# A two-layer decoder step on one core: the MLP's up projections as one level of Strassen's product, with squared relu and residual kept in memory

## The chip, the core and the metric

The kernel runs on one core of one Trainium2 chip. The metric is the time of one execution in device microseconds (us); three runs of the kernel before took 3162.02 us in the median, 3161.73 to 3175.02. The core has five engines that work side by side and meet through semaphores: TensorE (PE in the profile, with its weight loads as PEld), VectorE (DVE), ScalarE (ACT), GpSimd (POOL) and SyncE (SP), which here only issues DMAs. On-chip data lie in SBUF; matmul results lie in PSUM, in eight banks that the program hands out as three of `pg`, three of `pm` and two of `ps2`. "Memory" below is the chip's main memory, reached by DMA.

## The reference

A step of a decoder with two layers over 1032 tokens (1024 of a prompt, 8 of running sequences), D = 1024, all in float32. Layer 0 mixes with a gated delta rule and retention, layer 1 with an SSD mixer; after each mixer stands the same MLP with a hidden width of 4096:

```python
def squared_relu_mlp(h, w1, w2):
    a = jax.nn.relu(jnp.einsum('bld,df->blf', h, w1))
    return jnp.einsum('blf,fd->bld', a * a, w2)
...
    for layer in range(DEPTH):
...
        x = x + out
        x = x + squared_relu_mlp(rms_norm(x, norm_mlp[layer]), mlp_w1[layer], mlp_w2[layer])
```

The change concerns the last line, twice: the product with w1, the squared relu, and the product with w2 onto the residual.

## The kernel before

Data lie transposed: features on the 128 partitions, the T = 1032 tokens along the free axis, in three slices of NW = 344 (`NSL`). Float32 products are made of three matmuls in a reduced format: every operand is split into a high part (a rounded copy) and a low part (the rest), and `mm3` (L146) multiplies high by high, high by low and low by high into the same bank. Weights come through `load_w` (L134): SP loads a raw tile of 128x512 (three buffers), ACT casts the high part (L142), and DVE or POOL subtracts it for the low part (L143).

`out_proj` (L1332) ends the mixer. It loads the residual from memory (`accd`) into eight tiles `acc` (L1339), adds the projection's products into them slice by slice (L1346), and with `split_piece` makes `xh` and `xl`, the high and low parts of the normed residual without its token-wise factor. That factor, rstd, is made by `rstd_from` while the first up tile runs (matmuls at L259, L279 and L295, copies on ACT at L272 and L275), and is applied after the first product, at the relu.

`mlp` (L1221) then runs 32 hidden tiles of 128 features. `up(t)` calls `gemm_tile`: 8 slices of K x 3 token slices x 3 = 72 matmuls of 344 columns into three banks, evicted by relu times rstd on DVE (L1227), the square's high part on ACT (L1228), the square itself on POOL (L1229) and its low part on DVE (L1230). The hidden tiles stay in SBUF, in 14 buffers of `a2`. After every fourth up tile (the first one counted apart) `down(b)` takes four of them through `gemm_flush`: 8 output tiles x 3 token slices x 12 = 288 matmuls of 344 columns, each slice added into `acc` by DVE (L1238). The order on each engine is the order in which these Python loops issue; nothing reorders them. An engine runs its queue in that order, and a waiting instruction holds all behind it. In layer 1 the last block is `finish`, which also does the final norm.

Of the kernel before, what the change touches and what calls it, by code (L numbers as in the profile page):

```python
# [10 lines left out]
F32 = mybir.dt.float32  # L11
# [3 lines left out]
ALU = mybir.AluOpType  # L15
# [53 lines left out]
SHF = 8  # L69
RATE = (0.5, 0.6, 1.5, 0.5, 0.6)  # L70
# [25 lines left out]
class Kern:  # L96
# [327 lines left out]
    def layer(self, l):  # L424
        tc = self.tc
        nk = 16 if l else 8
        with ExitStack() as es:
# [5 lines left out]
            self.spill = [dp.tile([P, SEQ], F32, name=f"spill{l}_{k}") for k in range(nk)]  # L433
            self.egd = dp.tile([32, SEQ], F32, name=f"egd{l}")
# [4 lines left out]
            with ExitStack() as es_op:  # L439
# [9 lines left out]
                ap = es.enter_context(tc.tile_pool(name=f"acc{l}", bufs=1, side="right", reuse_waits="tile"))  # L449
# [763 lines left out]
    def mlp(self, l, acc, last):  # L1213
        nc, tc, I = self.nc, self.tc, self.I
        with tc.tile_pool(name=f"mlp{l}", bufs=1, reuse_waits="tile") as tp:
# [3 lines left out]
            def up(t):  # L1219
                hi = tp.tile([P, T], F32R, tag="a2", name="ahi", bufs=14)  # L1220
                lo = tp.tile([P, T], F32R, tag="a2", name="alo", bufs=14)  # L1221
                parts[t] = (hi, lo)

                def ev(n, ps):
                    s = NSL[n]
                    r = tp.tile([P, NW], F32, tag="r", name="r", bufs=4)
                    nc.vector.scalar_tensor_tensor(out=r, in0=ps, scalar=0.0, in1=self.rstd_bc[:, s], op0=ALU.max, op1=ALU.mult)  # L1227
                    nc.scalar.activation(hi[:, s], r, AF.Square)  # L1228
                    nc.gpsimd.tensor_tensor(out=r, in0=r, in1=r, op=ALU.mult)  # L1229
                    nc.vector.tensor_tensor(out=lo[:, s], in0=r, in1=hi[:, s].bitcast(F32), op=ALU.subtract)  # L1230
                self.gemm_tile(I["w1"][l, t], 128, ev, t == 1)

            def down(b):
                ks = range(4 * b, 4 * b + 4)
# [8 lines left out]
                for _ in self.gemm_flush(lambda m: I["w2"][l, b, m], [parts.pop(k) for k in ks], ev):  # L1243
                    pass
            def finish(b):
# [3 lines left out]
                for m in range(KT):  # L1249
                    dst = None  # L1250
                    if m < 5:
                        w = tp.tile([P, T], F32R, tag="a2", name="wfin", bufs=14)
                        dst = (w[:, 0:512], w[:, 512:1024])
# [78 lines left out]
    def out_proj(self, name, blocks, acc, tp, parts, norm):  # L1332
# [3 lines left out]
        with tc.tile_pool(name="oq" + name, bufs=1, side="right", reuse_waits="tile") as tq:  # L1336
# [3 lines left out]
            for i in range(1, len(blocks)):  # L1340
# [3 lines left out]
                def ev(m, n, ps):  # L1344
                    o = acc[m][:, NSL[n]]
                    nc.vector.tensor_tensor(out=o, in0=o, in1=ps, op=ALU.add)  # L1346
                    if last:
                        self.split_piece(m, n, o, ssq, tp, norm)
# [563 lines left out]
```

## Time and profile before

| what | value |
|---|---|
| median of three runs | 3162.02 us |
| the profiled execution | 3163.67 us, span in the trace 3161.5 us |
| TensorE clock granted over the span | 0.972 |
| MLP of layer 0 in the trace | about 779 to 1509 us |
| MLP of layer 1 in the trace | from about 2412 us nearly to the end |

The profile shows one execution. Its first part gives each engine's busy time and share of the span; the second cuts the span into 40 slices and gives busy tenths. The windows view gives, for chosen stretches, each engine's busy time with the number of instructions that began there, then the TensorE clock granted, the DMA engines' busy share and GB/s. In rows of groups the numbers are the count, busy time, mean duration in ns, then idle time before them with its releaser. A source view gives the least, middle and greatest duration of one line's instructions in ns.

### The profile page before, as it was taken

How to read it: one execution, taken by the hardware profiler on the slowest of the kernel's cores; microseconds unless marked ns; L12 is line 12 of the kernel's file. 1: busy time of each engine (PE TensorE's matmuls, PEld its weight loads, DVE VectorE, ACT ScalarE, POOL GpSimd, SP SyncE). 2: the span in 40 equal slices, each digit the busy share in tenths (PEclk: the TensorE clock that was granted, in tenths of full speed). 3: DMA queues.
4: the chain of work that ended last, by engine and by line, in shares of the span. 5: the costliest groups of instructions: out<-in, count | busy, mean ns of one | idle time of the engine just before them, and what ended most of it. 6: DMA issues, size and time to landing. Idle time of an engine off the chain costs nothing. (4 is left out here: it accounts for less than half of the span.)

```text
span 3161.5 us, 48870 instructions
## 1 busy us (share of the span) xinstructions
PE 3039.6 (96%) x19702; PEld 2918.4 (92%) x19702; DVE 1672.0 (53%) x3191; ACT 830.1 (26%) x1573; POOL 914.0 (29%) x928
## 2 busy tenths in 40 slices
PE   8999999989999999999998999998899999999998
PEld 6888888878999999999997989898899999999998
DVE  7664657554333333334788696968435333333334
ACT  4222222213211111113343434343124111111112
POOL 2121114114222112224135445445224222221124
PEclk9899989889999999999999999999999999999999
DMA  4011103153111111112222232324721111111112
GB/s 128 21 49 55 48 22 109 56 179 107 44 47 47 47 47 47 47 47 77 73 66 76 74 103 76 96 75 136 255 74 44 47 47 47 47 47 47 47 47 71
DMA packets 119186, 223.32 MB, mean 71 GB/s; under 512 B 14064, under 2 KB 43504, under 8 KB 118960
## 3 DMA queue, kind: packets, MB, share of 16 engines
q1 hardware_dynamic: 110512, 190.80, 19.9%
q0 software_dynamic: 8448, 29.40, 2.4%
q8 instruction: 155, 2.54, 0.3%
q14 instruction: 71, 0.58, 0.1%
HBM read 174.78 MB, written 43.24 MB: 69 GB/s over the span
## 5 line engine op out<-in xcount | busy, mean ns | idle before, releaser
L148 PE MATMUL pg<-xh,whi 128*128 128x344 f32 x3072 | 1000.9, 326 | 6.2 <-DVE z L1495 3.2
L150 PE MATMUL pg<-xh,wlo 128*128 128x344 f32 x3072 | 997.5, 325 | 0.7 <-DVE wlo L143 0.7
L149 PE MATMUL pg<-xl,whi 128*128 128x344 f32 x3072 | 997.1, 325 | 0.0
L148 PEld LDWEIGHTS pg<-xh,whi 128*128 128x128 f32 x3072 | 584.8, 190 | 13.0 <-DVE z L1495 3.7
L142 ACT CAST whi<-raw 128x512 fp32r<-128x512 f32 (+2 forms) x443 | 270.8, 611 | 1234.6 <-PE pg L149 1174.2
L150 PEld LDWEIGHTS pg<-xh,wlo 128*128 128x128 f32 x3072 | 584.8, 190 | 4.8 <-DVE wlo L143 1.7
L149 PEld LDWEIGHTS pg<-xl,whi 128*128 128x128 f32 x3072 | 583.6, 190 | 3.5 <-issue 2.1
L149 PE MATMUL pg<-alo,whi 128*128 128x344 f32 (+2 forms) x1476 | 472.4, 320 | 0.0
L150 PE MATMUL pg<-ahi,wlo 128*128 128x344 f32 (+2 forms) x1476 | 472.3, 320 | 0.0
L148 PE MATMUL pg<-ahi,whi 128*128 128x344 f32 (+2 forms) x1476 | 471.5, 319 | 0.0
L1238 DVE TENSOR_TENSOR acc<-acc,pg 128x344 f32<-128x344 f32 x360 | 182.9, 511 | 388.1 <-PE pg L150 388.1
L143 POOL TENSOR_TENSOR wlo<-raw,whi 128x512 fp32r<-128x512 f32 (+2 forms) x179 | 225.2, 1260 | 507.7 <-ACT whi L142 502.9
L1229 POOL TENSOR_TENSOR r<-r 128x344 f32<-128x344 f32 x192 | 146.1, 761 | 755.1 <-ACT ahi L1228 707.4
L143 DVE TENSOR_TENSOR wlo<-raw,whi 128x512 fp32r<-128x512 f32 x264 | 189.7, 719 | 190.4 <-ACT whi L142 182.6
L150 PEld LDWEIGHTS pg<-ahi,wlo 128*128 128x128 f32 x1476 | 277.6, 188 | 0.0
L148 PEld LDWEIGHTS pg<-ahi,whi 128*128 128x128 f32 x1476 | 277.5, 188 | 0.0
L149 PEld LDWEIGHTS pg<-alo,whi 128*128 128x128 f32 x1476 | 277.3, 188 | 0.0
L1230 DVE TENSOR_TENSOR alo<-r,ahi 128x344 fp32r<-128x344 f32 x192 | 134.5, 701 | 253.8 <-POOL r L1229 253.8
L1228 ACT ACTIVATE ahi<-r 128x344 fp32r<-128x344 f32 x192 | 94.5, 492 | 340.9 <-DVE r L1227 340.9
L148 PE MATMUL pg<-mhi,whi 128*128 128x344 f32 x408 | 133.2, 326 | 9.9 <-DVE acc L1346 7.1
L1227 DVE SCALAR_TENSOR_TENSOR r<-pg,rstd_bc 128x344 f32<-128x344 f32 x186 | 94.8, 510 | 79.4 <-PE pg L150 78.1
L150 PE MATMUL pg<-mhi,wlo 128*128 128x344 f32 x408 | 132.8, 326 | 0.0
(539 smaller groups left out, 4191.6 us busy)
## 6 DMA issues: line engine op xcount, KB each, us to landing
raw<-w SPq DMA_DIRECT2D x256, 256.0 KB, 2.6
raw<-wis SPq DMA_DIRECT2D x80, 256.0 KB, 2.8
raw<-wih SPq DMA_DIRECT2D x56, 256.0 KB, 2.8
mraw<-spill SPq DMA_DIRECT2D x17, 512.0 KB, 4.5
accd<-ost SPq DMA_DIRECT2D x48, 172.0 KB, 3.1
acc<-accd SPq DMA_DIRECT2D x16, 516.0 KB, 7.3
EG<-egd SPq DMA_DIRECT2D x32, 256.0 KB, 6.7
dS<-sstate SPq DMA_DIRECT2D x32, 256.0 KB, 7.1
```

Of the source, the lines that this page charges most:

```text
L142: nc.scalar.copy(hi[:, :n], raw[:, :n])
L143: (lo_eng or nc.vector).tensor_tensor(out=lo[:, :n], in0=raw[:, :n], in1=hi[:, :n].bitcast(F32), op=ALU.subtract)
L148: t.matmul(ps, lhsT=whi, rhs=xhi, start=start, stop=False)
L149: t.matmul(ps, lhsT=whi, rhs=xlo, start=False, stop=False)
L150: t.matmul(ps, lhsT=wlo, rhs=xhi, start=False, stop=stop)
L1227: nc.vector.scalar_tensor_tensor(out=r, in0=ps, scalar=0.0, in1=self.rstd_bc[:, s], op0=ALU.max, op1=ALU.mult)
L1228: nc.scalar.activation(hi[:, s], r, AF.Square)
L1229: nc.gpsimd.tensor_tensor(out=r, in0=r, in1=r, op=ALU.mult)
L1230: nc.vector.tensor_tensor(out=lo[:, s], in0=r, in1=hi[:, s].bitcast(F32), op=ALU.subtract)
L1238: nc.vector.tensor_tensor(out=s, in0=s, in1=ps, op=ALU.add)
```

## The change

The up projections of a layer are regrouped. Hidden tiles t and t + 16 form a pair; together with the two halves of K (slices 0 to 3 and 4 to 7) and with tokens cut in two halves, a pair is a product of 2x2 blocks. One level of the Strassen product in Winograd's form replaces eight block products by seven, of sums of weight blocks with sums of token blocks. Tokens are cut into four quarters of 258, so a pair is two calls of `pair`, for quarters 0 and 1 and for quarters 2 and 3, of seven products each; a product is 4 slices of K x 3 = 12 matmuls of 258 columns. Tiles 0 and 16 remain plain.

```diff
-            self.mlp(l, acc, l == 1)
+            self.mlp_up(l)
+            ap = es.enter_context(tc.tile_pool(name=f"res{l}", bufs=1, side="right", reuse_waits="tile"))
+            acc = [ap.tile([P, T], F32, name=f"res{l}_{m}") for m in range(KT)]
+            for m in range(KT):
+                nc = self.nc
+                nc.sync.dma_start(acc[m], self.accd[m])
+            self.mlp_down(l, acc, l == 1)
...
+            def out(t, cols, r, n):
+                v.scalar_tensor_tensor(out=r, in0=r, scalar=0.0, in1=self.rstd_bc[:, cols], op0=ALU.max, op1=ALU.mult)
+                a.activation(r, r, AF.Square)
+                nc.gpsimd.dma_start(self.hid[t][:, cols], r)
...
+            plain(0, False)
+            with tc.tile_pool(name=f"upx{l}", bufs=1, side="right", reuse_waits="tile") as xp:
+                for k in range(4):
+                    x = []
+                    for m in (k, k + 4):
+                        r = xp.tile([P, T], F32, tag="x", name="ux", bufs=4)
+                        nc.sync.dma_start(r, self.accd[m])
+                        a.activation(r, r, AF.Copy, scale=self.V(norm, m))
+                        x.append(quarters(r))
...
+                    for j, x0, x1, e in ((1, b12, b11, v), (2, b22, t[1], g), (3, b22, b12, v), (4, t[2], b21, g)):
+                        e.tensor_tensor(out=t[j], in0=x0, in1=x1, op=ALU.subtract)
+                    for j in (2, 1, 3, 4):
+                        hi, lo = TB[j][k]
+                        a.copy(hi, t[j])
+                        v.tensor_tensor(out=lo, in0=t[j], in1=hi.bitcast(F32), op=ALU.subtract)
+            plain(HT, True)
...
+            def weights(t):
...
+                a11, a12 = load(t, 0), load(t, 1)
+                W[1] = parts(a11)
+                W[2] = parts(a12)
+                a21 = load(t + HT, 0)
+                s3 = total(a11, a21, ALU.subtract)
+                d = total(a21, a11, ALU.subtract)
+                a22 = load(t + HT, 1)
+                s2 = total(d, a22, ALU.add)
+                W[6] = parts(s2)
+                s4 = total(a12, s2, ALU.subtract)
+                s1 = s2
+                g.tensor_tensor(out=a21, in0=a21, in1=a22, op=ALU.add)
+                W[5] = parts(a21)
+                W[7] = parts(s3)
+                W[4] = parts(a22)
+                W[3] = parts(s4)
+                return W
...
+                c1 = add(a, None, prod(1), None)
+                add(v, r0[:, L], prod(2), c1)
+                u2 = add(v, None, prod(6), c1)
+                c5 = add(a, None, prod(5), None)
+                u3 = add(v, None, prod(7), u2)
+                u4 = add(g, None, c5, u2)
+                add(g, r1[:, R], c5, u3)
+                p4 = prod(4)
+                add(v, r1[:, L], u3, p4, ALU.subtract)
+                out(t + HT, cols, r1, 516)
+                add(v, r0[:, R], prod(3), u4)
+                out(t, cols, r0, 516)
+            W = weights(1)
+            for t in range(1, HT):
+                pair(t, W, 0)
+                nxt = weights(t + 1) if t + 1 < HT else None
+                pair(t, W, 1)
+                W = nxt
```

In this diff v is DVE, a is ACT, g is POOL. `parts` casts a weight block on ACT (L1290 of the changed kernel) and subtracts for its low part on DVE (L1291); `total` is a sum on POOL (L1303; the sum into a21 is L1318). `add` with one operand copies a bank on ACT (L1340), with two it adds on the named engine (L1342). `out` is L1238 to L1240: relu times rstd on DVE over 516 tokens, square on ACT, and a store to `hid` in memory from POOL's queue. The residual takes a way through memory too: `out_proj` stores each finished `acc[m]` (L1526, SP), the token sums and, after the up stage, `res` read it back (L1262, L459).

At pair 5 hidden tiles 0 and 1 are read back and split into quarters of `xh` and `xl` that no product reads any more (L1371 to L1375). `mlp_down` begins with them: `begin` runs 8 x 4 x 6 = 192 matmuls of 258 columns, the first real block then has only two tiles, and `fetch` brings the other hidden tiles from memory (L1385), casts them on ACT (L1388) and takes their low parts on DVE (L1389), into 16 buffers of `a2`:

```diff
-            for t in range(HID):
-                up(t)
-                if t % 4 == 0 and t:
-                    down(t // 4 - 1)
+            for k in (2, 3):
+                fetch(k)
+            begin()
+            for b in range(HID // 4 - 1):
+                for k in range(4 * b + 4, 4 * b + 8):
+                    fetch(k)
+                down(b, 0 if b else 2)
```

On ACT, at the end of layer 0's output projection, `sq` being the square of the last residual piece, the queue before reads:

```order
L241 ACTIVATE sq_7562<-acc0_7_6935 128x344
L142 CAST whi_7776<-raw_7774 128x512
L272 COPY rstd_bc_70<-pm_7649 128x512
L275 COPY rstd_bc_70<-pm_7685 128x8
L272 COPY rstd_bc_70<-pm_7667 128x512
L1228 ACTIVATE ahi_7570<-r_7688 128x344
L1228 ACTIVATE ahi_7570<-r_7705 128x344
```

and now (`ux` is the residual read back, `sa` a token sum, `t10h` to `t40h` their high parts, `r` the hidden tile 0):

```order
L242 ACTIVATE sq_7601<-acc0_7_6967 128x344
L143 CAST whi_7934<-raw_7932 128x512
L1263 ACTIVATE ux_7798<-ux_7798,vec_68 128x1032
L1263 ACTIVATE ux_7801<-ux_7801,vec_68 128x1032
L273 COPY rstd_bc_70<-pm_7720 128x512
L276 COPY rstd_bc_70<-pm_7756 128x8
L1271 CAST t10h_7611<-sa_7804 128x516
L1271 CAST t20h_7619<-sa_7805 128x516
L273 COPY rstd_bc_70<-pm_7738 128x512
L1247 ACTIVATE r_7759<-r_7759 128x344
```

Two scalings of the residual read back have come ahead of the copies of rstd, and casts of token sums among them.

On POOL, in the middle of the up stage, a row holds the same instruction as often as xN says. Before, around a down block, the queue has squares and low parts of weights:

```order
L1229 TENSOR_TENSOR r<-r 128x344 x8
L143 TENSOR_TENSOR wlo<-raw,whi 128x512
L1229 TENSOR_TENSOR r<-r 128x344
L143 TENSOR_TENSOR wlo<-raw,whi 128x512
L1229 TENSOR_TENSOR r<-r 128x344 x2
L143 TENSOR_TENSOR wlo<-raw,whi 128x512
L1229 TENSOR_TENSOR r<-r 128x344
L143 TENSOR_TENSOR wlo<-raw,whi 128x512 x5
```

Now, for the pair 5 (`c` and `r` are the parts of its outputs, `sa` and `raw` the weight sums of pair 6):

```order
L1342 TENSOR_TENSOR c<-c 128x258
L1342 TENSOR_TENSOR r<-c 128x258
L1303 TENSOR_TENSOR sa<-raw 128x512 x2
L1240 DMA hid_21_128<-r 128x516
L1240 DMA hid_5_112<-r 128x516
L1303 TENSOR_TENSOR sa<-sa,raw 128x512
L1318 TENSOR_TENSOR raw<-raw 128x512
L1303 TENSOR_TENSOR sa<-raw,sa 128x512
```

The squares and low parts are gone from POOL; the sums of the next pair's weights stand between the output sums and the stores of the pair at hand.

On SP, at the end of the up stage, loads have come that were not there: the residual, and hidden tiles between the weights of w2. Before, SP loads only weights there.

```order
L1298 DMA raw<-w 128x512 x31
L139 DMA raw<-w 128x256 x6
L459 DMA res_0_12075<-accd_0_140 128x1032
L459 DMA res_1_12076<-accd_1_141 128x1032
L459 DMA res_2_12077<-accd_2_142 128x1032
```

Behind them come the other five `res` loads, then hidden tiles 2 and 3, then again weights.

More of the change, by code (lines that the diff above doesn't have):

```diff
@@ L69 @@
 SHF = 8
+A2 = 16
 RATE = (0.5, 0.6, 1.5, 0.5, 0.6)
@@ L433, in layer @@
             self.spill = [dp.tile([P, SEQ], F32, name=f"spill{l}_{k}") for k in range(nk)]
+            self.hid = [dp.tile([P, T], F32, name=f"hid{l}_{k}") for k in range(HID)]
             self.egd = dp.tile([32, SEQ], F32, name=f"egd{l}")
@@ L1214, in mlp, with mlp_down @@
+    def mlp_down(self, l, acc, last):
         nc, tc, I = self.nc, self.tc, self.I
@@ L1217, in mlp, with fetch, begin, down @@
             parts = {}
[L1219 to L1234, printed above, removed]
+            def fetch(k):
+                raw = tp.tile([P, T], F32, tag="hraw", name="hraw", bufs=2)
+                nc.sync.dma_start(raw, self.hid[k])
+                hi = tp.tile([P, T], F32R, tag="a2", name="ahi", bufs=A2)
+                lo = tp.tile([P, T], F32R, tag="a2", name="alo", bufs=A2)
+                nc.scalar.copy(hi, raw)
+                nc.vector.tensor_tensor(out=lo, in0=raw, in1=hi.bitcast(F32), op=ALU.subtract)
+                parts[k] = (hi, lo)
+            def begin():
+                for m in range(8):
+                    hi, lo = self.load_w(I["w2"][l, 0, m][:, 0:256], 256, nc.gpsimd)
+                    for j in range(4):
+                        n = slice(258 * j, 258 * j + 258)
+                        ps = self.pg()[:, :258]
+                        for k in range(2):
+                            c = slice(258 + 516 * (j % 2), 516 + 516 * (j % 2))
+                            s = slice(k * 128, k * 128 + 128)
+                            i = 2 * k + j // 2
+                            self.mm3(ps, hi[:, s], lo[:, s], self.xh[i][:, c], self.xl[i][:, c], k == 0, k == 1)
+                        nc.vector.tensor_tensor(out=acc[m][:, n], in0=acc[m][:, n], in1=ps, op=ALU.add)
+            def down(b, k0=0):
+                ks = range(4 * b + k0, 4 * b + 4)
                 def ev(m, n, ps):
@@ L1242, in ev @@
                             nc.gpsimd.dma_start(self.resd[m], acc[m])
-                for _ in self.gemm_flush(lambda m: I["w2"][l, b, m], [parts.pop(k) for k in ks], ev):
+                for _ in self.gemm_flush(lambda m: I["w2"][l, b, m][:, k0 * 128:], [parts.pop(k) for k in ks], ev):
                     pass
@@ L1251, in finish @@
                     if m < 5:
-                        w = tp.tile([P, T], F32R, tag="a2", name="wfin", bufs=14)
+                        w = tp.tile([P, T], F32R, tag="a2", name="wfin", bufs=A2)
                         dst = (w[:, 0:512], w[:, 512:1024])
@@ L1348, in ev @@
                         self.split_piece(m, n, o, ssq, tp, norm)
+                        if n == 2:
+                            nc.sync.dma_start(self.accd[m], acc[m])
                 for _ in self.gemm_flush(lambda m: self.I[name][m, :, c0 * 128:c0 * 128 + w], cur, ev):
```

79 lines of the change are left out of this document (77 added, 2 removed).

## The prediction

> **What bounds the kernel now.** I read the page's busy times and its slices first, then the windows view over the two MLP stages.
>
> ```profile
> PE 3039.6 (96%) x19702; PEld 2918.4 (92%) x19702; DVE 1672.0 (53%) x3191; ACT 830.1 (26%) x1573; POOL 914.0 (29%) x928
> ...
> PE   8999999989999999999998999998899999999998
> ```
>
> ```profile
> core 0: us, PE busy (x) PEld busy (x) DVE busy (x) ACT busy (x) POOL busy (x), PEclk, DMA share, GB/s
> 790.00:1500.00 710.00, 710.00 (x4512) 709.83 (x4513) 257.43 (x461) 142.14 (x261) 172.57 (x181) 1.00 0.17 50
> 2425.00:3095.00 670.00, 670.00 (x4261) 670.00 (x4260) 233.31 (x416) 119.04 (x212) 145.67 (x152) 1.00 0.16 46
> 900.00:1000.00 100.00, 100.00 (x638) 100.00 (x637) 33.93 (x63) 18.57 (x33) 21.28 (x23) 1.00 0.16 46
> ```
>
> TensorE is busy for all of both windows at clock 1.00, while VectorE works 36% of the first (257.43 of 710), ACT 20%, POOL 24%. Nothing but the number of matmuls and their pitch bounds the MLP. The pitch (start to start) of a matmul of 344 columns: 100 us / 638 = **156.7 ns** (the window with the most matmuls per us; missing records would only make it look longer). For fewer columns the final projection has rows:
>
> ```profile
> 3133.06 0.28 PE L148 MATMUL pg<-ahi,wfin 128*128 128x256 f32 x1
> ...
> 3135.77 0.28 PE L150 MATMUL pg<-ahi,wfin 128*128 128x256 f32 x1
> ```
>
> These are the first and last of 24 matmuls of 256 columns, each with weights of its own: 2.71 us / 23 = 117.8 ns. The slope between the two widths is (156.7 - 117.8) / 88 = 0.44 ns a column, so 258 columns cost **118.7 ns**, an estimate two columns away from a measured width.
>
> **The change on TensorE.** Before, one layer's MLP is 32 up tiles of 72 matmuls and 8 down blocks of 288, all of 344 columns: 4608 x 156.7 ns = 722.1 us. After, two up tiles stay (144 matmuls); the other 30 become 15 pairs of 2 x 7 products x 4 slices x 3 = 168 matmuls of 258. The down projection keeps 2160 matmuls of 344, and its first 144 become 192 of 258 in `begin`. Per layer 2304 x 156.7 + (2520 + 192) x 118.7 = 361.0 + 321.9 = 682.9 us: **39.2 us less**, all of it from the pairs (22.56 us before, 19.94 after, 2.6 saved, 15 times; `begin` is even: 22.8 against 22.6).
>
> **What the pairs need beside TensorE.** Durations come from these rows of the lines and source views:
>
> ```profile
> L142 ACT CAST whi<-raw 128x512 fp32r<-128x512 f32 x419 | 259.4, 619 | 1179.4 <-PE pg L149 1134.8 <-PE ps L149 14.0 <-issue 13.5
> L143 POOL TENSOR_TENSOR wlo<-raw,whi 128x512 fp32r<-128x512 f32 x155 | 202.8, 1308 | 430.4 <-ACT whi L142 425.5 <-DMA accd<-ost 4.4 <-PE pg L149 0.4
> L1754 POOL DMA_DIRECT2D o_sssm<-dS x32 | 18.5, 577 | 44.2 <-DVE dS L1753 44.2
> ```
>
> ```profile
> L143 DVE TENSOR_TENSOR wlo<-raw,whi x264: 669/692/1921, 10.1 to 3078.4; 128x512 fp32r<-128x512 f32 x132
> ...
> L143 POOL TENSOR_TENSOR wlo<-raw,whi x179: 731/1289/2292, 606.5 to 3106.2; 128x512 fp32r<-128x512 f32 x155, 128x384 fp32r<-128x384 f32 x16, 128x256 fp32r<-128x256 f32 x8
> ```
>
> ```profile
> L421 DVE SCALAR_TENSOR_TENSOR z<-th,z x48: 677/690/1529, 85.6 to 2216.0; 128x516 f32<-128x516 f32 x48
> ```
>
> ```profile
> L420 ACT ACTIVATE th<-z x48: 622/635/639, 83.8 to 2213.8; 128x516 f32<-128x516 f32 x48
> ```
>
> ```profile
> L1306 DVE TENSOR_TENSOR acc<-acc,pg x24: 410/548/564, 3101.5 to 3146.8; 128x392 f32<-128x392 f32 x8, 128x384 f32<-128x384 f32 x8, 128x256 f32<-128x256 f32 x8
> ```
>
> ```profile
> L1311 ACT ACTIVATE sqf<-acc x21: 416/525/536, 3102.6 to 3147.3; 128x392 f32<-128x392 f32 x7, 128x384 f32<-128x384 f32 x7, 128x256 f32<-128x256 f32 x7
> ```
>
> In each source row the three numbers are the least, middle and greatest duration; the least of the last two rows and of POOL's is that of 256 columns, which I take for 258. Per pair, in us:
> - DVE: seven low parts of weights 7 x 0.69, ten evictions 10 x 0.42, four relu steps of 516 columns 4 x 0.69: **11.8**.
> - ACT: seven casts 7 x 0.62, four copies 4 x 0.42, four squares 4 x 0.64: **8.6**.
> - POOL: five sums of 128x512 5 x 1.29, four of 258 columns 4 x 0.74, four DMA issues 4 x 0.58: **11.7**.
>
> Each is well under the pair's 19.9 us of TensorE. But the weights of the next pair are a chain. From the start of a pair, a product being 12 x 0.1187 = 1.42 us: products 1, 2, 6, 5, 7 end at 7.1, DVE's u3 at 7.5, POOL's r1 at 8.3; behind it POOL makes s3 and d, to 10.9; d frees the buffer of a11, the a22 load (2.6 us, row below) lands at 13.5, s2 ends at 14.8, a21+a22 at 16.1, s4 at 17.4. Weight 6 is cast and has its low part at 14.8 + 0.62 + 0.69 = 16.1, the last, weight 3, about 20 (five low parts in DVE's queue between evictions). TensorE wants weight 6 as the third product of the next pair, at 19.9 + 2.8 = 22.7, and weight 3 as its seventh, at 28.4. Over 6 us of slack: no stall, if nothing stretches. The new stores put a wait into POOL's queue: a store stands there until DVE's relu step (0.69) and ACT's square (0.64) are through, and behind it queue s2 and s4; the first half's two stores are due by 8.5 + 0.42 + 1.33 = 10.3 and 11.7, and two issues end at 12.3, before a22 has landed: covered.
>
> What may stretch it stands in the trace:
>
> ```profile
> 3096.53 1.59 DVE L1230 TENSOR_TENSOR alo<-r,ahi 128x344 fp32r<-128x344 f32 x1 [1.48 <-POOL r L1229]
> ```
>
> ```profile
> 3096.45 1.29 POOL L143 TENSOR_TENSOR wfin<-raw,wfin 128x512 fp32r<-128x512 f32 x1
> ```
>
> ```profile
> L1230 DVE TENSOR_TENSOR alo<-r,ahi x192: 504/518/1639, 793.3 to 3100.0; 128x344 fp32r<-128x344 f32 x192
> ```
>
> The DVE subtraction that began 0.08 us after a POOL one took 1.59 us where the middle one takes 0.518: it stood still nearly until POOL was through. In a pair DVE's 7 + 4 instructions on SBUF alone (7.6 us) and POOL's nine (9.4) add to 17.0 even if none overlap, under 19.9, so I add nothing in the forecast and keep the case in which the rest doesn't interleave either as a rival.
>
> The Trainium skill, "SBUF — State Buffer", section "Who interferes with whom", says that a VectorE instruction with two SBUF inputs and a GpSimd instruction that reads SBUF exclude each other for the whole instruction, and that a VectorE instruction with at most one SBUF input does not. The 1.59 us row agrees with it; by that rule every meeting in the new up stage would cost what this row shows, which is the second rival below.
>
> **Entry of the up stage (new wait).** The sums of tokens need the normed residual, which now goes to memory and back. On SP's queue each store of a piece waits for its last add; the weight loads of both plain tiles stand ahead of the last store, behind it only loads for the first pair and the loads back. Rows for it:
>
> ```profile
> L259 PE MATMUL pm<-ones_r,rstd_bc x54: 212/275/317, 779.7 to 2414.9; 128*128 128x56 f32 x54
> ```
>
> ```profile
> L272 ACT COPY rstd_bc<-pm x8: 586/587/588, 47.0 to 2424.3; 128x512 f32<-128x512 f32 x8
> ```
>
> ```profile
> L1228 ACT ACTIVATE ahi<-r 128x344 fp32r<-128x344 f32 x192 | 94.5, 492 | 340.9 <-DVE r L1227 340.9
> ```
>
> ```profile
> acc<-accd SPq DMA_DIRECT2D x16, 516.0 KB, 7.3
> ...
> resd<-acc POOLq DMA_DIRECT2D x8, 516.0 KB, 4.1
> ```
>
> ```profile
> raw<-w SPq DMA_DIRECT2D x256, 256.0 KB, 2.6
> ```
>
> ```profile
> L226 ACT ACTIVATE xh<-xr,vec x8: 1139/1156/1158, 6.1 to 23.5; 128x1032 fp32r<-128x1032 f32 x8
> ```
>
> Count from the last add of the output projection. The last residual piece is stored (4.1 us), and by the program's semaphores the second load back waits for it and lands at about 9.5 (4.1 to 7.3 more). ACT has then 7 x 1.16 (scaling, 128x1032) + 16 x 0.62 (casts of token sums) + 6 x 0.49 (squares of the two plain tiles) + 2 x 0.59 (copies of rstd) + 2 x 0.62 (weights 1 and 2) = 23.4 us in its queue ahead of the first product: about 33. TensorE is covered only by the two plain tiles and the rstd products, 2 x 72 x 0.1567 + 18 x 0.12 + 8 x 0.12 = 25.7 us (the rstd products overlap; 0.12 is the pitch of 256 columns). It waits about 7 us, and then about 3 more for weight 6, whose sums stand on POOL behind eight token sums: **+10 us per layer** (5 if the loads come early, 16 if DVE and POOL block each other there). The wait may also lower the clock:
>
> ```profile
> 725.68 0.63 PE L148 MATMUL pg<-mhi,whi 128*128 128x344 f32 x1 [4.51 <-DVE acc L1346]
> ```
>
> ```profile
> 724.00:728.00 4.00, 2.32 (x8) 2.35 (x9) 2.53 (x6) 2.43 (x6) 0.00 (x0) 0.51 1.00 376
> 728.00:732.00 4.00, 4.00 (x19) 4.00 (x18) 1.46 (x3) 1.20 (x3) 0.05 (x1) 0.64 1.02 413
> ```
>
> After the 4.51 us wait, the granted clock (the third figure from the end) was 0.51 and 0.64 in the two windows of 4 us. Half speed for the first two products costs about 3 us, but weight 6 is the later one there, so it lies inside the 10.
>
> **Seam between up and down.** The residual loads (eight of 516 KB) and the first four hidden tiles come through one SP queue; the loads into reused space wait for the last pair. The first eviction of `begin` needs the first of them, some 5 us after the last product, with three banks of six matmuls (3 x 0.71 us) as cover: 3 us. Four low parts stand among its evictions:
>
> ```profile
> L468 DVE TENSOR_TENSOR mlo<-mraw,mhi x17: 1218/1234/2508, 687.1 to 2329.3; 128x1032 fp32r<-128x1032 f32 x17
> ```
>
> An eviction behind one waits 1.2 us, half of which the banks hide, say 1 us in all: **+4 us** (1 to 8). Later down blocks load two hidden tiles ahead of their use, under 45 us of matmuls: nothing. The old evictions of the up tiles and POOL's squaring go from engines that bound nothing: 0.
>
> **Sum.** -39.2 + 10 + 4 = -25 per layer, -50 for two. The profiled execution took 3163.67 us: 3163.67 - 50 = 3113.5. It stands 1.65 above the median of 3162.02, so against the median the forecast is **3112 us** (-1.6%).
>
> **Rivals.**
> - *Entry and seams hidden.* If the loads back land early enough that ACT never queues, the whole 78 us is kept: 3084. For it: DVE and POOL idle there; against it: ACT's 23.4 us is a plain sum behind one landing. 12%.
> - *Exclusion between DVE and POOL.* If they never overlap, a pair takes 11.8 + 9.4 = 21.2 us instead of 19.94: 30 x 1.3 = 39 lost, 3151. For it the 1.59 us row; against it that ten of DVE's instructions read PSUM, and that the middle low part is unstretched. 18%.
> - *Slower: the weight chain is the loop.* If POOL also stands idle for each last-quarter load (2.6 us), as its sums cannot start a pair ahead with three raw buffers, a pair takes 21.2 + 2.6 = 23.8 us: 30 x 3.9 = 116 lost on top, 3228. It turns the sign once a pair takes over 19.94 + 50 / 30 = 21.6 us. Against it: weights 1 and 2 are made a pair early and the chain has 6 us of slack. 8%.
> - *The pitch does not shrink in proportion.* If 258 columns cost 130 ns instead of 118.7, 5424 matmuls cost 61 us more: 3173, no gain. Against it stand the 256-column rows, which also change weights each time. 7%. Where it is less than the line says, 115 ns, the gain grows by 20.
>
> **Numbers.** The forecast case has 55%, with 3092 to 3138 as its own range (entry 5 to 16, seam 1 to 8, pitch off by 2 ns). About 0.5%, 16 us, is what a measurement of this kernel can tell from no change. Faster by more: 55 + 12 + 5 (part of the exclusion case, and of the pitch) = 72%; within: 17%; slower: 8% and the worst of the others, 11%. The range leaves out the slower case and the far ends of the pitch: from 3080 (the hidden case, less the 4 us that 0.7 ns of pitch make) to 3160 (the exclusion case plus the upper end of the seams).
>
> **What would show it.** The windows view in the pairs should have TensorE at 100% with some 840 matmuls per 100 us, a pair every 20 us; an idle time of 5 to 10 us ahead of the first L1290 weights, released by ACT or by DVE's low part; a second of a few us at `begin`, released by a residual load. If pairs come every 21 to 24 us with TensorE waiting for a low part of weight 6, 5 or 3, the exclusion or the chain was underrated. If there is no wait and the time is still above 3130, the pitch is wrong. Low parts of the weights (L1291) with a middle duration near 0.69 speak for my reading, near 1.5 for exclusion.

## The result, and the profile after

The changed kernel takes **3178.22 us** in the median of 14 runs (3172.33 to 3188.14) against 3161.90 for the kernel before in runs beside it: 1.0053 times as long, with a 95% interval of 1.0040 to 1.0066. The forecast was 3112, 1.6% faster. The profiled execution took 3178.02 us; its page begins:

```profile
span 3176.2 us, 52465 instructions
...
PE 2993.6 (94%) x20518; PEld 2857.3 (90%) x20518; DVE 1927.4 (61%) x3509; ACT 988.4 (31%) x1855; POOL 1188.2 (37%) x1170
```

TensorE's busy time fell by 46 us (3039.6 to 2993.6) and the span still grew by 14.7: the matmuls did get cheaper, and more than the gain went into waiting. The windows view cuts the MLP of layer 0 into its parts: plain tiles up to the first pair, 15 pairs, `begin`, the rest of the down projection.

```profile
core 0: us, PE busy (x) PEld busy (x) DVE busy (x) ACT busy (x) POOL busy (x), PEclk, DMA share, GB/s
777.90:813.04 35.14, 25.09 (x162) 23.89 (x160) 28.51 (x44) 22.98 (x38) 18.33 (x15) 0.92 0.55 178
813.04:1143.40 330.36, 313.86 (x2520) 308.29 (x2521) 201.56 (x320) 111.10 (x229) 189.43 (x197) 0.98 0.30 99
1143.40:1172.20 28.80, 25.45 (x195) 24.83 (x194) 17.33 (x37) 7.93 (x13) 7.71 (x9) 0.94 0.78 271
1172.20:1516.40 344.20, 343.49 (x2180) 342.29 (x2179) 152.58 (x251) 88.00 (x141) 105.84 (x92) 1.00 0.32 100
```

The same stage of the kernel before, in one window:

```profile
779.70:1510.70 731.00, 730.32 (x4644) 728.70 (x4643) 269.69 (x489) 150.68 (x279) 182.75 (x192) 1.00 0.18 52
```

So the stage went from 731.0 to 738.5 us. The prediction wanted the change between the windows to be -25. Where it went is read from the pitch that undisturbed matmuls have (0.120 us for 258 columns, from a run below; 670 us / 4261 = 0.1572 for 344, from the row of before):

| part of layer 0 | matmuls alone, us | taken, us | lost | forecast of the loss |
|---|---|---|---|---|
| entry: 2 plain tiles and rstd | 144 x 0.1572 + 3.1 = 25.7 | 35.1 | 9.4 | 7 |
| 15 pairs | 2520 x 0.120 = 302.4 | 330.4 | **28.0** | 3 (the first pair's weight 6) |
| `begin` | 192 x 0.120 = 23.0 | 28.8 | 5.8 | 4 |
| down projection | 2180 x 0.1572 = 342.7 | 344.2 | 1.5 | 0 |

The pairs hold most of the surprise, but not all that is lost in them has one cause. A windows view cuts them at the first matmul of product 4 in the pairs 1, 6 and 7:

```profile
813.04:827.15 14.11, 10.67 (x60) 9.88 (x61) 9.04 (x12) 4.25 (x8) 6.82 (x6) 0.73 0.25 82
827.15:932.85 105.70, 102.93 (x842) 101.43 (x841) 67.57 (x104) 35.66 (x74) 62.05 (x64) 1.00 0.30 101
932.85:959.91 27.06, 22.30 (x170) 21.68 (x169) 15.91 (x26) 10.16 (x20) 14.08 (x14) 0.94 0.34 109
959.91:1143.40 183.49, 177.96 (x1454) 175.31 (x1453) 109.04 (x180) 61.03 (x128) 106.48 (x115) 1.00 0.29 99
```

By the program these are 60, 840, 168 and 1452 matmuls, at 0.120 us each 7.2, 100.8, 20.2 and 174.2 us. So 6.9 us are lost at the head of the first pair, which still belongs to the entry (the granted clock is 0.73 there); 6.9 us in the one step from pair 6 to pair 7, where the reload of hidden tiles 0 and 1 falls; and 4.9 + 9.3 = 14.2 us in the other pairs, about 1.1 us in each of 13 steps. The entry as a whole then lost 9.4 + 6.9 = 16.3 us, where 10 were forecast.

TensorE's rows in the pairs, taken from the timeline (start, duration, instruction, and in brackets the wait ahead of it with its releaser), show its waits:

```profile
813.04 0.58 PE L149 MATMUL pg<-xh,whi 128*128 128x258 f32 x1 [8.61 <-ACT whi L1290]
816.41 0.58 PE L151 MATMUL pg<-xh,wlo 128*128 128x258 f32 x1 [2.26 <-DVE wlo L1291]
...
904.41 0.39 PE L149 MATMUL pg<-xh,whi 128*128 128x258 f32 x1 [0.48 <-ACT c L1340]
...
925.52 0.39 PE L149 MATMUL pg<-xh,whi 128*128 128x258 f32 x1 [0.47 <-ACT c L1340]
...
944.12 0.58 PE L149 MATMUL pg<-t10h,whi 128*128 128x258 f32 x1 [3.90 <-ACT c L1340]
```

The first two are the entry. The next two are one and the same place in two successive pairs, 21.11 us apart, where a pair of matmuls alone takes 168 x 0.120 = 20.2 us: something beside TensorE has a period of 21.1 us here (some steps take 22). The last one comes once a layer, behind the reload of hidden tiles 0 and 1.

What has that period can be read from POOL's timeline in one pair:

```profile
910.71 3.01 POOL L1303 TENSOR_TENSOR sa<-raw 128x512 f32<-128x512 f32 x2 [1.33 <-DMA raw<-w]
913.66 1.09 POOL L1240 DMA_DIRECT2D hid<-r  x2
917.06 1.28 POOL L1303 TENSOR_TENSOR sa<-sa,raw 128x512 f32<-128x512 f32 x1 [2.31 <-DMA raw<-w]
918.31 1.28 POOL L1318 TENSOR_TENSOR raw<-raw 128x512 f32<-128x512 f32 x1
919.54 1.28 POOL L1303 TENSOR_TENSOR sa<-raw,sa 128x512 f32<-128x512 f32 x1
920.78 0.74 POOL L1342 TENSOR_TENSOR c<-c 128x258 f32<-128x258 f32 x1
921.49 0.74 POOL L1342 TENSOR_TENSOR r<-c 128x258 f32<-128x258 f32 x1
```

and ACT's right behind it:

```profile
923.03 0.63 ACT L1239 ACTIVATE r<-r 128x516 f32<-128x516 f32 x1 [9.29 <-DVE r L1238]
924.05 0.64 ACT L1239 ACTIVATE r<-r 128x516 f32<-128x516 f32 x1 [0.38 <-DVE r L1238]
924.59 0.60 ACT L1290 CAST whi<-sa 128x512 fp32r<-128x512 f32 x1
925.10 0.36 ACT L1340 COPY c<-pg 128x258 f32<-128x258 f32 x1
```

POOL waits for the load of a21, makes s3 and d, waits 2.31 us for the load of a22 (which needs a11's buffer), makes s2 and two more sums, and only then the output sums of the pair at hand (L1342); DVE's relu waits for these, ACT's squares for the relu, the cast of weight 6 stands behind the squares, and the copy that frees TensorE's bank stands behind the cast (925.10, for the wait at 925.52). The casts of the other weights and their low parts follow, and the low part of weight 4 frees the buffer into which the next a21 is loaded:

```profile
927.71 1.24 DVE L1291 TENSOR_TENSOR wlo<-raw,whi 128x512 fp32r<-128x512 f32 x1
```

It ends at 928.95, and POOL's next sum, which waits for that load, begins at 932.32. The chain closes on itself. Two of its links are longer here than alone, as DVE and POOL met (last section): s3 and d took 3.01 us instead of 2 x 1.28, the low part of weight 4 1.24 instead of 0.69. Together that is 1.0 us, as much as the turn exceeds TensorE's 20.2 us by. A chain without these meetings would thus take some 20.1 us and stop nothing; this is an estimate from the rows, as no run takes the meetings away and leaves the chain. POOL waits for loads twice per pair, by the source view of the weight loads:

```profile
POOL sa L1303: 111.8, 56
```

111.8 us in 56 waits: 28 pairs, 2.0 us each time.

### The profile page after: what moved, and what is told of

Its sections match the earlier page's. It is cut to its first block, busy times and chain, and to the rows that moved or that the text cites. A ratio compares the mean times of both kernels' runs of the same rounds, so it can differ in the third digit from the quotient of the medians.

```text
span 3176.2 us, 52465 instructions
## 1 busy us (share of the span) xinstructions
PE 2993.6 (94%) x20518; PEld 2857.3 (90%) x20518; DVE 1927.4 (61%) x3509; ACT 988.4 (31%) x1855; POOL 1188.2 (37%) x1170
## 5 line engine op out<-in xcount | busy, mean ns | idle before, releaser
L149 PE MATMUL pg<-xh,whi 128*128 128x344 f32 (+1 forms) x2240 | 720.1, 321 | 44.0 <-ACT whi L1290 16.9
L151 PE MATMUL pg<-xh,wlo 128*128 128x344 f32 (+1 forms) x2240 | 710.4, 318 | 6.4 <-DVE wlo L1291 4.5
L150 PE MATMUL pg<-xl,whi 128*128 128x344 f32 (+1 forms) x2240 | 710.0, 317 | 0.0
L149 PEld LDWEIGHTS pg<-xh,whi 128*128 128x128 f32 x2240 | 429.4, 192 | 61.4 <-ACT whi L1290 17.5
L149 PE MATMUL pg<-ahi,whi 128*128 128x344 f32 (+1 forms) x1380 | 441.9, 320 | 1.9 <-DVE res L1411 1.9
L151 PE MATMUL pg<-ahi,wlo 128*128 128x344 f32 (+1 forms) x1380 | 442.2, 320 | 0.0
L150 PE MATMUL pg<-alo,whi 128*128 128x344 f32 (+1 forms) x1380 | 440.9, 320 | 0.0
L151 PEld LDWEIGHTS pg<-xh,wlo 128*128 128x128 f32 x2240 | 429.3, 192 | 11.7 <-DVE wlo L1291 5.1
L150 PEld LDWEIGHTS pg<-xl,whi 128*128 128x128 f32 x2240 | 429.3, 192 | 3.4 <-issue 2.1
L1411 DVE TENSOR_TENSOR res<-res,pg 128x344 f32<-128x344 f32 x360 | 182.4, 511 | 322.8 <-PE pg L151 321.9
L1238 DVE SCALAR_TENSOR_TENSOR r<-r,rstd_bc 128x516 f32<-128x516 f32 x120 | 103.5, 863 | 110.2 <-POOL r L1342 107.6
L1291 DVE TENSOR_TENSOR wlo<-raw,whi 128x512 fp32r<-128x512 f32 x120 | 126.3, 1054 | 1.9 <-ACT whi L1290 1.5
```

Source lines behind the costliest of these rows:

```text
L149: t.matmul(ps, lhsT=whi, rhs=xhi, start=start, stop=False)
L150: t.matmul(ps, lhsT=whi, rhs=xlo, start=False, stop=False)
L151: t.matmul(ps, lhsT=wlo, rhs=xhi, start=False, stop=stop)
L1238: v.scalar_tensor_tensor(out=r, in0=r, scalar=0.0, in1=self.rstd_bc[:, cols], op0=ALU.max, op1=ALU.mult)
L1291: v.tensor_tensor(out=lo, in0=x, in1=hi.bitcast(F32), op=ALU.subtract)
L1411: nc.vector.tensor_tensor(out=s, in0=s, in1=ps, op=ALU.add)
```

## The experiments

LOOP is the theory just read: three raw buffers close the weight chain, and its length is the period. EXCLUSION is the rival of the prediction: DVE and POOL hold each other up, and this sets the pace. Times are medians; ratios are to the kernel before on the same chip, which took 3160 to 3163 us in the median on each of them.

**A raw buffer of its own for a22.**

```diff
-                    raw = self.wp.tile([P, 512], F32, tag="raw", name="raw", bufs=3)
+                    raw = wr.tile([P, 512], F32, tag="raw4", name="raw", bufs=1) if kh and tt >= HT else self.wp.tile([P, 512], F32, tag="raw", name="raw", bufs=3)
```

> Change against the changed kernel: the last quarter a22 of a pair's weights gets a raw buffer of its own, so that the three others no longer take turns with it; nothing else. Theory LOOP: a pair takes 21.1 us instead of 20.2 because its weight chain closes on itself (the low part of weight 4 frees the buffer for the next a21, load 2.8 us, s3, d, load of a22 3.3 us, s2, two more sums, two output sums, relu, squares, cast of weight 6, then the other casts and low parts). Then pairs come every 20.2 to 20.5 us, the 0.64 us wait of TensorE ahead of each second half's first product is gone, and the kernel takes 28 x 0.7 = 20 us less than 3178: about 3158. Theory EXCLUSION: DVE and POOL hold each other up and that alone sets 21.1 us; it is as strong here, so pairs stay at 21 us and the time at 3173 to 3180. The wait after pair 5 and the entry stay under both.

3148.53 us, ratio 0.9958 (0.9942 to 0.9975). The windows view, pairs behind the reload:

```profile
965.00:1110.00 145.00, 145.00 (x1208) 144.88 (x1207) 97.73 (x151) 53.52 (x108) 88.96 (x96) 1.00 0.30 102
```

TensorE is busy throughout; 145 us / 1208 = 0.120 us, 20.2 us a pair, with POOL as busy as before. Ahead of the reload (845 to 925, 658 matmuls) a pair still takes 20.4. 30 us went, where LOOP expected 20: the 14.2 us that the pairs outside entry and reload lose in a layer make some 28 in two, more than the expectation's 0.7 us a pair. EXCLUSION as what alone sets the pace falls; as a part of the chain's length it stands.

**The five weight sums on DVE.**

```diff
-                    g.tensor_tensor(out=o, in0=x, in1=y, op=op)
+                    v.tensor_tensor(out=o, in0=x, in1=y, op=op)
...
-                g.tensor_tensor(out=a21, in0=a21, in1=a22, op=ALU.add)
+                v.tensor_tensor(out=a21, in0=a21, in1=a22, op=ALU.add)
```

> Change against the changed kernel: the five weight sums of a pair run on DVE instead of POOL; three raw buffers as before. LOOP: the chain gets shorter by 5 x 0.6 us and by the 0.5 us that a POOL sum lost beside DVE, to 17.5 us, so TensorE sets the pace (20.2 us a pair) and the time falls to about 3153. EXCLUSION: the nine POOL instructions of a pair become four, the low parts of the weights (middle now near 0.7 to 1.2 us) all take 0.69, pairs at 20.2 us, also about 3153. A third possibility, HEAD OF LINE: a sum that waits for the a22 load now holds DVE's queue, with the evictions of the products behind it, for up to 3 us; TensorE then waits for banks, pairs stay at 21 us or more, time 3175 to 3200.

3134.92 us, ratio 0.9919 (0.9904 to 0.9934): better than both numbers expected, and the third possibility fell. From the second pair of layer 0 to the last:

```profile
840.00:1100.00 260.00, 260.00 (x2166) 260.00 (x2165) 191.51 (x338) 102.20 (x197) 71.04 (x104) 1.00 0.32 109
```

260 / 2166 = 0.120 us, no wait at all, the one behind the reload included. Since this shortens the chain and takes POOL away at once, it doesn't tell the two theories apart; the next two were meant to.

**The sum s4 computed twice, with the loop closed and with a22's own buffer.**

```diff
                 s4 = total(a12, s2, ALU.subtract)
+                g.tensor_tensor(out=s4, in0=a12, in1=s2, op=ALU.subtract)
```

> Change against the changed kernel: POOL computes the weight sum s4 a second time into the same buffer (1.28 us more of POOL per pair, no new result). LOOP: this stands inside the chain that closes over the three raw buffers, so each pair gets longer by all of it, 21.1 to about 22.4 us, 28 x 1.28 = 36 us: about 3214. If POOL and DVE are merely busy beside TensorE (no loop), POOL works 13 of 21 us and the addition costs 0 to 10 us: 3178 to 3188.

> The same second s4 on POOL, but with the raw buffer of its own for a22 (the kernel that took 3148.5). LOOP: with the chain open the 1.28 us are covered, pairs stay at 20.2 us, time 3146 to 3153 (a few us at the entry and the reload at most). EXCLUSION: POOL's extra 1.28 us stop DVE as much as before, 5 to 36 us more: 3154 to 3185.

In the changed kernel the second sum costs 30.1 us (3208.32, ratio 1.0143, 1.0105 to 1.0181) for 28 x 1.28 = 36 us on POOL, which in the changed kernel worked only 189.43 of 330.36 us in the pairs: 84% of it lands on the end. In the pairs themselves all of it does: the 13 steps of layer 0 without the reload take 22.54 us in the mean, against 21.25. So POOL is not merely busy beside TensorE (3178 to 3188). EXCLUSION isn't refuted by it, as 5 to 36 us for the same addition would be its range too. Its waits view has the new place of waiting:

```profile
PE pg L149 <- DVE r L1343: 33.4, 23, 2.3
```

With a22's own buffer it should have cost nothing and cost 19.3 us (3167.87, ratio 1.0020, 0.9998 to 1.0042). The windows before and behind the reload:

```profile
845.00:925.00 80.00, 77.10 (x631) 75.91 (x630) 58.17 (x84) 29.30 (x60) 49.96 (x53) 1.00 0.31 106
970.00:1110.00 140.00, 139.38 (x1154) 138.57 (x1153) 99.41 (x142) 48.11 (x98) 92.95 (x96) 1.00 0.29 101
```

80 / 631 x 168 = 21.3 us a pair in the first, 140 / 1154 x 168 = 20.4 in the second (20.2 in the first three steps, 20.5 to 20.8 later). LOOP's expectation (3146 to 3153) failed, and the time lies in EXCLUSION's range. One reading keeps LOOP: the buffer takes one load out of the chain, but the other three raw buffers still turn, and the period is then so little under TensorE's 20.2 us that it has no room for 1.28 more. That isn't shown. POOL's waits for loads don't show it: they are 109.0 us in 26 waits here and 113.0 in 26 in the kernel without the second sum, whose pairs take 20.2 us. The same addition can't be told from EXCLUSION by its time alone.

**The reload through its own buffer.**

```diff
-                            r = tp.tile([P, 516], F32, tag="r", name="r", bufs=3)
+                            r = tp.tile([P, 516], F32, tag="rr", name="r", bufs=1)
```

> Change against the changed kernel: the four halves of hidden tiles 0 and 1 that are read back after pair 5 go through a buffer of their own instead of the three that the pairs' outputs use. If the wait there (4.1 us, then 0.85 us and some half-clock matmuls, 6 us a layer) comes from output buffers that the reload occupies, it goes: 12 us less, about 3166. If it comes from the order of the queues (the cast and the low part of the reload stand on ACT and DVE ahead of the copy and sums of the next products and wait for a store and a load of the same data), it stays within 1 us a layer, time 3175 to 3180.

3175.67 us, ratio 1.0045 (1.0030 to 1.0060): the wait stayed, and moved from pair 6 to pairs 2 and 3, with the place that the reload has in the queues. ACT's timeline shows what it is:

```profile
861.90 0.62 ACT L1374 CAST xh<-r 128x516 fp32r<-128x516 f32 x1 [8.46 <-DMA r<-hid]
863.94 0.64 ACT L1239 ACTIVATE r<-r 128x516 f32<-128x516 f32 x1 [1.42 <-DVE r L1238]
```

ACT stands 8.46 us for a load of the reload, with the squares and casts of the pair queued behind. SP's timeline shows why that load was late:

```profile
843.73 15.05 SPq L1298 DMA_DIRECT2D raw<-w  x4
858.89 0.37 SPq L1371 DMA_DIRECT2D r<-hid  x1
```

It stood behind four loads of weights, over which SP's queue spent 15.05 us. So it is the order of the queues, SP's as much as ACT's. The run is no clean test of the buffers at the old place, as the edit moved the reload and left it one buffer.

**Entry: eight buffers for token sums, and token sums on DVE alone.** The second is an edit of the kernel with weight sums on DVE.

```diff
-                    t = {j: temp().rearrange("p (g n) -> p g n", g=2) for j in range(1, 5)}
+                    t = {j: xp.tile([P, 516], F32, tag="sx", name="sx", bufs=8).rearrange("p (g n) -> p g n", g=2) for j in range(1, 5)}
```

```diff
-                    for j, x0, x1, e in ((1, b12, b11, v), (2, b22, t[1], g), (3, b22, b12, v), (4, t[2], b21, g)):
+                    for j, x0, x1, e in ((1, b12, b11, v), (2, b22, t[1], v), (3, b22, b12, v), (4, t[2], b21, v)):
```

> Change against the changed kernel: the token sums at the entry of the up stage have eight buffers instead of the four they share with the weight sums. If the four buffers hold the next slice's sums back until the low parts of the slice before are through, the wait ahead of the first pair (8.6 + 2.3 us) falls to about 5: 10 to 12 us less over both layers, about 3167. If ACT's queue sets it (the forecast's reason) nothing changes: 3178. If DVE and POOL excluding each other sets it (sums on POOL 1.5 us, low parts on DVE 1.6 us where they meet), at most 2 us a layer change.

> Against the kernel with weight sums on DVE (3134.9): the eight token sums that POOL made at the entry of each up stage go to DVE too, so that at the entry nothing of POOL stands beside DVE but stores. If DVE and POOL excluding each other sets the entry (sums on POOL 1.5 us, low parts beside them 1.6 to 1.7 us), the 8.8 us wait ahead of the first pair gets shorter by about 8 x (1.5 + 0.9 - 0.69) / 2 = 7 us a layer: about 3122. If ACT's queue sets it (the forecast's reason: 23.4 us behind the landing of the second load), the wait stays at 8 to 9 us: 3133 to 3137.

3178.03 us (1.0056, 1.0035 to 1.0078) and 3134.14 (0.9907, 0.9871 to 0.9942): neither moves the time, as both texts expected if ACT's queue set the entry. With the sums on DVE the wait only takes another shape, 6.47 us at the second product instead of 8.60 at the first. What both leave unchanged shows in two windows of the changed kernel:

```profile
785.00:800.00 15.00, 13.83 (x87) 13.05 (x87) 13.45 (x20) 11.55 (x19) 7.69 (x7) 1.00 0.66 212
800.00:815.00 15.00, 5.54 (x32) 4.95 (x30) 15.00 (x18) 10.70 (x17) 9.29 (x7) 0.74 0.19 60
```

DVE is busy 28.45 of these 30 us (held times included), ACT 22.25, and in the second half 15.00 against 10.70. So it is DVE's sums and low parts that fill the entry; ACT's casts wait for them in turn. With all sums on DVE it was still busy 27.29 of 30 (window of that run from 788 to 818): what POOL no longer holds up, the added sums take. No run took work off DVE there, so that it alone sets the length is read from these windows and not tested.

**Two more plain tiles.** Tiles 1 and 17 plain, 14 pairs; both edits on the kernel with weight sums on DVE. First behind the token sums, then all four ahead of them:

```diff
             plain(HT, True)
+            plain(1, False)
+            plain(HT + 1, True)
...
-            W = weights(1)
-            for t in range(1, HT):
+            W = weights(2)
+            for t in range(2, HT):
```

> Against the kernel with weight sums on DVE (3134.9): hidden tiles 1 and 17 are plain too, so four plain tiles stand ahead of the first of 14 pairs. A pair of tiles costs 144 x 0.1575 = 22.7 us instead of 20.2, 2.5 us more a layer; it covers the whole wait at the entry (8.8 + 1.0 + 2.1 us and about 3 us of half-clock matmuls behind it, 15 a layer in all). Expected 2 x (15 - 2.5) = 25 us less: about 3110. If the wait merely moves behind the new tiles (the token sums are late because DVE serves the plain tiles first), it keeps 4 us or more of it: 3115 to 3130.

> Against the kernel with weight sums on DVE (3134.9): four plain tiles again (0, 16, 1, 17), but all four are written ahead of the token sums, so that the casts of their weights no longer stand behind the sums on ACT and DVE, which made TensorE wait 8.6 us ahead of tile 1 in the last run. If the wait at the entry is only the sums' length of about 35 us against 25.7 us of cover, it goes: 13 us less and 2.5 more per layer, about 3113. If the token sums are now served so late that the first pair waits for them again, 5 us a layer or more of it stay: 3120 to 3132.

3131.47 us (0.9907, 0.9881 to 0.9933), above both numbers expected, and **3121.27** (0.9871, 0.9836 to 0.9907), 14 us less than without the plain tiles where the better case had 22. In the first the wait came ahead of tile 1, behind 72 + 72 matmuls as ever:

```profile
828.19 0.66 PE L149 MATMUL pg<-xh,whi 128*128 128x344 f32 x1 [8.60 <-ACT whi L143]
```

The cast of tile 1's weights stood behind the token sums on ACT. With the four tiles written first, the only wait over 0.7 us in layer 0's up stage is one of 1.43 us, so the wait at the entry did go, as the first case had it, though the time is in the second's range (3120 to 3132):

```profile
826.06 0.36 PE L149 MATMUL ps<-t20h,whi 128*128 128x258 f32 x1 [1.43 <-DVE r L1246]
```

**The seam, and all together.** On the kernel with weight sums on DVE, `begin` takes its banks from all eight; then that with four plain tiles first and with `fetch` of tiles 2 and 3 called inside `begin`.

```diff
-                        ps = self.pg()[:, :258]
+                        ps = next(banks)()[:, :258]
```

> Against the kernel with weight sums on DVE (3134.9): the first block of the down projection takes its banks from all eight instead of three. If the wait at the seam is the residual's way back (the first eviction waits for its landing, three banks cover 2.1 us), only its first part (0.5 us and what half clock follows) goes: 1 us a layer, 3133. If the evictions that stand behind the low parts of the hidden tiles make up the second part (1.4 + 1.3 us late in this block), that goes too: 4 us a layer, 3127. If the second part is ACT's queue (the casts of hidden tiles wait for their loads, behind eight residual loads, and hold the casts of weights), it stays: 3133.

> The changes that helped, together: weight sums on DVE, four plain tiles ahead of the token sums, eight banks in the first block of the down projection, and hidden tiles 2 and 3 fetched inside that block instead of ahead of it. Sum of what each should save against 3134.9: 22 + 2 x 3 = 28 us: about 3107, 1.7% under the kernel before. If the entry keeps its wait: 3125.

3140.32 us (0.9930, 0.9909 to 0.9951), no gain over 3134.92, and 3118.21 (0.9859, 0.9822 to 0.9896), not to be told from 3121.27 and short of the 3107 expected. More banks don't help, as the longer wait there is for a cast of w2. In the changed kernel ACT's rows show what that cast stands behind, 1.67 us being TensorE's wait for it at 1163.23:

```profile
1160.43 1.05 ACT L1388 CAST ahi<-hraw 128x1032 fp32r<-128x1032 f32 x1 [7.12 <-DMA hraw<-hid]
1161.76 1.05 ACT L1388 CAST ahi<-hraw 128x1032 fp32r<-128x1032 f32 x1 [0.28 <-DMA hraw<-hid]
1162.72 1.01 ACT L143 CAST whi<-raw 128x256 fp32r<-128x256 f32 x3
```

The wait is still there in the combined kernel, and longer:

```profile
1130.42 0.58 PE L149 MATMUL pg<-xh,whi 128*128 128x258 f32 x1 [3.50 <-ACT whi L143]
```

The edit of the fetches didn't cure it. In the kernel of the eight banks alone the wait for a residual load is gone and ACT is the releaser of the one left (1.67 us), so the third expectation has the place right; its time is 7 us above the 3133 expected, which stays unexplained. What would set it right wasn't found.

**POOL's sums with both cures.** a22's own buffer and the four plain tiles first, weight sums on POOL.

> Against the kernel with a raw buffer of its own for a22 (3148.5; weight sums still on POOL): four plain tiles ahead of the token sums as well. It tells how much of what is left DVE and POOL excluding each other makes. If the open chain and the covered entry are all there is, pairs run at 20.2 us with POOL at its sums, and the time is that of the same kernel with the sums on DVE: 3121 (3115 to 3127). If exclusion has a price of its own, the pairs after the first, the reload after pair 5 and the token sums stay late: 3130 to 3140.

3135.38 us (0.9914, 0.9897 to 0.9930), 14 us above the same with sums on DVE and inside the range that the text gives for a price of EXCLUSION (3130 to 3140). Pairs behind the reload:

```profile
955.00:1100.00 145.00, 145.00 (x1207) 144.81 (x1206) 97.36 (x150) 53.12 (x108) 87.34 (x95) 1.00 0.29 99
```

145 / 1207 x 168 = 20.2 us with POOL at its sums: with the chain open, exclusion has no price in the running pairs. The difference sits at the reload, where these two waits and the slow matmuls behind them take 8 us a layer that the kernel with sums on DVE doesn't lose:

```profile
926.81 0.38 PE L149 MATMUL ps<-t40h,whi 128*128 128x258 f32 x1 [2.04 <-DVE r L1344]
...
942.10 0.36 PE L149 MATMUL pg<-xh,whi 128*128 128x258 f32 x1 [3.04 <-DVE r L1344]
```

There it has one. The eviction that ends the second wait began at 941.54, behind these two of DVE, which stood beside POOL's weight sums:

```profile
938.19 1.75 DVE L1238 SCALAR_TENSOR_TENSOR r<-r,rstd_bc 128x516 f32<-128x516 f32 x1 [3.92 <-POOL r L1344]
939.87 1.75 DVE L1293 TENSOR_TENSOR wlo<-raw,whi 128x512 fp32r<-128x512 f32 x1
```

Alone they take 0.70 and 0.69 us, so some 2.1 of the 3.04 us are theirs (an estimate); the 3.92 us ahead of them are the wait for an output sum on POOL, which stood behind two weight sums and their load.

## Why the prediction was wrong, point by point

- **What bounds the MLP, and the matmuls' gain: right, slightly too large.** The pitch of 258 columns is 0.120 us, not 118.7 ns; that of 344 over a long stretch is 157.2, not 156.7. So 4608 - 2304 of the wide ones less 2712 of the narrow is 362.2 - 325.4 = 36.8 us a layer instead of 39.2.
- **The pairs: here it failed.** The step "Over 6 us of slack: no stall, if nothing stretches" is wrong in three ways.
  - I let the chain begin with POOL's queue and counted only the wait of a22 for a11's buffer, and not that a21's load waits for the low part of weight 4 of the pair before, which closes the chain over three raw buffers; a rival at 8% ("the weight chain is the loop") named the three buffers and POOL's idle time, but not this link.
  - I measured its slack to the wrong consumer: the third product of the next pair, at 22.7. The copy queued right behind weight 6's cast frees the bank of that pair's first product and is wanted 2.8 us earlier, at 19.9.
  - I let the cast of weight 6 follow s2 at once, with the output sums of the pair's first half ahead of s3, at 8.3. In the rows these are made at 920.78, 16.4 us after the pair's start at 904.41 and behind all the weight sums. s2 ends at 13.9, earlier than my 14.8; but the cast of weight 6 begins only at 20.2 (924.59), because it stands behind ACT's squares, which wait for DVE's relu, which waits for these output sums. I had the 6.3 us between at nothing.

  The loop cost 14.2 us a layer where none was expected. It ran at 21.1 to 22 us a pair, 21.25 in the mean, instead of the rival's 23.8 and under the break-even of 21.6 that I gave; it is 14.2 of the 32.5 us a layer that were missed, the largest part, and the sign turned with the reload and the entry on top. The two runs that break or lengthen the chain show it (3148.53, 3208.32).
- **The reload behind pair 5: no term of the sum.** It is a wait that the change adds, and I didn't name what queues behind its cast. The step in which it falls lost 6.9 us, about 6 more than the others: the wait of 3.90 us and the slow matmuls behind it. ACT stood 6.17 us there for a load of the reload (cast at 941.01), and the rows of ACT and SP in the run above show the same and the weight loads ahead of it.
- **The entry: undersized, and the reason wrong.** The two long waits, 8.61 + 2.26 us, match my 7 + 3 by luck. The loss is 16.3 us, the upper end of my 5 to 16: the matmuls at half clock, which I counted as lying inside the 10, came on top, because the second wait was for the low part of weight 1, ahead of them, and not for weight 6 behind them (0.45 us). I added ACT's queue (23.4 us), took DVE and POOL as idle there in a rival, and left out that DVE's queue, at 16 low parts and eight sums held up by POOL, was longer. A window of the two engines there would have been the test; the two runs that move buffers and sums changed nothing, the one that covers the entry with plain tiles took it away.
- **The seam: right in size** (5.8 against 4), mostly for another reason: the wait for a residual load was 0.51 us; the casts of w2 on ACT stand behind a hidden tile's load.
- **Exclusion of DVE and POOL: wrong to put at nothing.** It sets no pace by itself: with the chain opened, pairs ran at 20.2 us beside POOL's sums. But it lengthens single instructions, and where these are links of the chain it lengthens the chain, here, by the estimate above, by the 1.0 us that it was too long. My own sign missed it. The middle duration of the low parts is near 0.69, as I said it would be if I was right, while the first two sums of a pair, which are links, have a middle of 1.69 against 1.29:

```profile
L1291 DVE TENSOR_TENSOR wlo<-raw,whi x120: 675/686/1817, 815.7 to 2766.1; 128x512 fp32r<-128x512 f32 x120
L1303 POOL TENSOR_TENSOR sa<-raw x60: 1287/1694/1785, 811.6 to 2750.1; 128x512 f32<-128x512 f32 x60
```

One sentence ahead of the prediction is wrong: the queues are not simply in the order in which the loops issue. The order rows show it themselves, with casts of token sums among the copies of rstd; instructions are also placed when the program is built, which fits that the reload moved when its buffer changed.

Two steps were not tried: the up stage with enough raw buffers for two pairs, which would tell the length of the rest of the loop; and the same chain without the meetings of DVE and POOL.

## What to carry to other kernels

Where a loop over few buffers passes several engines, follow the chain once round until it meets itself, load, sums, casts and what frees the first buffer, and compare that length with the bound engine's period; busy shares (61% on DVE, 57% on POOL, 34% on ACT in the pairs) say nothing of it. An instruction that is lengthened now and then counts in full where it is a link, whatever the middle duration of its kind. Measure slack to the first instruction queued behind the late one, on every queue that it holds, not to the product that reads its result. A doubled step inside the suspected loop is a cheap test, but not one that decides alone: here the pairs grew by all of it with the loop closed, and the kernel still by about half of it with the loop opened.

## What the runs showed of the hardware

DVE instructions with both inputs in SBUF and POOL sums that meet both get longer. In the POOL rows above the two sums at 910.71 took 3.01 us where two alone take 2 x 1.28, and DVE had beside them:

```profile
911.08 1.47 DVE L1238 SCALAR_TENSOR_TENSOR r<-r,rstd_bc 128x516 f32<-128x516 f32 x1
912.47 1.80 DVE L1291 TENSOR_TENSOR wlo<-raw,whi 128x512 fp32r<-128x512 f32 x1
...
917.75 0.42 DVE L1342 TENSOR_TENSOR r<-c,ps 128x258 f32<-128x258 f32 x1 [2.28 <-PE pm L151]
```

1.47 us instead of 0.70 and 1.80 instead of 0.69; the eviction from PSUM at 917.75, beside POOL's sum of 917.06, took its usual 0.42. The Trainium skill, "SBUF — State Buffer", section "Who interferes with whom", speaks of an exclusive hold by whoever issues first. The rows agree: the four instructions fill 3.56 us, from 910.71 to 914.27, nearly the sum of their times alone (3.95), and each lengthened one would be one that waited for its turn.

A wait of 0.48 us costs TensorE more than itself: at 904.41 the first matmul has 0.39 us where the others have 0.28, it starts 0.77 us after the one before it and the next 0.22 us after it, so the place takes 0.75 us of the pair. After the 3.90 us wait they started 0.21 us apart instead of 0.12 for some 3 us.
